# A paired SwiGLU up-projection on Trainium2: one matrix's products after the other's, and the fifth product in 512-column matmuls

## The chip, the cores and the metric

The kernel runs on one core of one Trainium2 chip. The metric is the device time of one execution in microseconds (us). The kernel before takes 1759.15 us, the median of three runs (1758.93 to 1760.65). Profiles and traces are of single executions. The engines are named as in the profile: PE (TensorE matmuls), PEld (its weight loads), DVE (VectorE), ACT (ScalarE), POOL (GpSimd) and SP (the queue that issues most DMAs).

## The reference

A decoder of two layers on 512 tokens of width 1024, all in float32. Each layer is a half-step feed-forward (FFN), a token mixer, a second half-step FFN and a norm:

```python
def swiglu(x, w1, w3, w2):
    return (jax.nn.silu(x @ w1) * (x @ w3)) @ w2
...
    for l in range(DEPTH):
        h = x + 0.5 * swiglu(rms_norm(x, ffn1_norm[l]), ffn1_w1[l], ffn1_w3[l], ffn1_w2[l])
...
        h = h + y @ w_out[l]

        h = h + 0.5 * swiglu(rms_norm(h, ffn2_norm[l]), ffn2_w1[l], ffn2_w3[l], ffn2_w2[l])

        x = rms_norm(h, final_norm[l])
```

There are four FFNs; w1 and w3 are 1024 x 2816, w2 is 2816 x 1024. The change touches the products `x @ w1` and `x @ w3` of the four FFNs only.

## The kernel before

**Precision.** Every float32 operand is cut into a high part and a low part, and a product is made of three: high x high, high x low, low x high. For a weight tile `split` (L147) does this: ACT copies the tile into the high part `whi` (L148), and DVE subtracts that from the tile and writes the low part `wlo` (L149).

**Blocks and quarters.** The 2816 hidden columns are 22 blocks of 128, f = 0 to 21. `ffn` (L475) does blocks 0 to 3 plainly. From block 4 on, two blocks are made at once by `up_pair` (L362), for w1 and w3 (i = 0 and 1) together. The blocks form quarters of 6, 6, 6 and 4; after a quarter's blocks (and one pair of the next quarter, made ahead) come its products with w2 (L546 to L564), which run from `mm` banks and add into `h`. Back to back stand therefore the pairs 4 and 6; 8, 10 and 12; 14, 16 and 18; and 20 alone. Pair 4 is called the first pair here (`f == PLAIN`).

**Seven products.** For a pair, one matrix's four quarter products (two blocks of columns, two halves of the 1024 rows, the tokens in halves of 256) are had from seven products instead of eight, over sums of weights and of operands. `Seven` (L297) holds the operand sums, once per FFN: in the traces' names `mh` and `ml` are those of products 1, 2 and 6, `xhi` those of 3 and 5, `xlo` those of 7 and 4. On the weights' side product 1 and 2 use the raw block f, 6 and 3 use sums of it, 7 and 5 use `X`, and 4 uses the raw block f + 1 (`z`).

- `X` (`wsum` in the traces) is loaded by SP (L369), and GpSimd then adds a second part into it with an accumulating DMA (L370). There are three `wsum` buffers and three `raw` buffers.
- `raw[i]` becomes the weights of 6 and 3 by two DVE additions in place (L443, L444 in the later pairs; L416, L417 in the first). The first of them reads `X[i]`.
- `unit` (L357) splits a tile that is used twice. `whi` and `wlo` have four buffers each.

**Two ways to write one product.** `product` (L377) makes 12 matmuls of 256 columns: for each of four k, the weight's high part with the operand's high part and then its low part; then four of the weight's low part. `beside` (L384) lets the operand's high and low parts, which lie side by side, pass in one matmul of 512 columns, four of these, then four of 256 columns for the weight's low part. It leaves two partial sums of 256 columns in a bank, which DVE adds (`summed`, L402). The later pairs make 2, 3, 7 and 4 with `beside`, and 1, 6 and 5 with `product`.

**Banks.** The eight PSUM banks are in named pools: `mm` 3, `cf` 1, `po` 2, `pt` 2. In the first pair products 1, 2, 6 and 5 are in two `po` banks (`xy`), and 3, 7 and 4 in two `pt` banks (`zv`). In a later pair products 1, 6 and 5 of each matrix share a `pt` bank (`x`), 2 and then 7 and 4 are in `po`, 3 in `cf` or `mm`. ACT copies products 1, 6 and 5 out of their bank into `part`.

**Order.** Each engine runs its instructions in order. A scheduler sets the order of each engine from the program and its own model; `queued` and `tc.issue_after` bind single places. In the code, a later pair makes 1 and 2 of both matrices (with each one's raw sums right behind), then 6 and 3 of both, then 7 and 5 of both, then 4 of both.

Of the kernel before, what the change touches and what calls it, by code (L numbers as in the profile page):

```python
# [13 lines left out]
AF = mybir.ActivationFunctionType  # L14
# [4 lines left out]
P = 128  # L19
D = 1024  # L20
S = 512
# [44 lines left out]
def trunk(ctx: ExitStack, tc: tile.TileContext, xT, memT, pos, w1a, w3a, w2a, w1b, w3b, w2b,  # L66
          wconv, wqk, wvm, wmem, wout, gains, small, rows, consts, out):
    nc = tc.nc
    V, G, A, T = nc.vector, nc.gpsimd, nc.scalar, nc.tensor
# [21 lines left out]
    def bank(shape, tag):  # L91

        if tag == "mm":
            return ps_mm.tile(shape, F32, tag=tag, name=tag)
        return ps_ax.tile(shape, F32, tag=tag, name=tag, bufs=1 if tag == "cf" else 2)

    def tm(name, tag="t", bufs=None):
        return tmp.tile([P, S], F32, tag=tag, name=name, **({"bufs": bufs} if bufs else {}))
# [4 lines left out]
    def raw_tile(src, cols):  # L103
        raw = wst.tile([P, UNIT], F32, tag="raw", name="raw", bufs=3)
        nc.sync.dma_start(raw[:, 0:cols], src)
        return raw
# [5 lines left out]
    first = []  # L112
# [34 lines left out]
    def split(hi, lo, x, on):  # L147
        a = A.activation(hi, x, AF.Copy)  # L148
        return a, on.tensor_tensor(out=lo, in0=x, in1=hi.bitcast(F32), op=ALU.subtract)  # L149
# [12 lines left out]
    def pair():  # L162
        return (wst.tile([P, UNIT], F32R, tag="whi", name="whi"), wst.tile([P, UNIT], F32R, tag="wlo", name="wlo"))
# [23 lines left out]
    def blk(k, n=P):  # L187
        return slice(k * n, (k + 1) * n)
# [97 lines left out]
    QW = 512  # L286
    QT = 256
# [65 lines left out]
    def gated():  # L353
        p = gated_pair()
        return [at(p, ALL, i, ALL) for i in range(2)]

    def unit(x):  # L357
        p = pair()
        split(p[0], p[1], x, V)
        return p  # L360

    def up_pair(l, w13, f, M):  # L362

        raw = [raw_tile(w13[i][l, f], D) for i in range(2)]
        X = []
        for i in range(2):

            x = wst.tile([P, UNIT], F32, tag="aux", name="wsum", bufs=3)
            nc.sync.dma_start(x.rearrange("p (f c) -> p f c", f=2), w13[i][l, f : f + 2, :, 0:QW].rearrange("f p c -> p f c"))  # L369
            G.dma_start(x, w13[i][l, f + 1], accum_op=ALU.add)  # L370
            X.append(x)
        z = wst.tile([P, UNIT], F32, tag="raw", name="raw", bufs=3)
        for i in range(2):
            nc.sync.dma_start(z[:, blk(i, QW)], w13[i][l, f + 1, :, QW:])
        x0, x1 = blk(0, QT), blk(1, QT)

        def product(ps, w, half, j, first=False):  # L377


            for n, (part, q) in enumerate([(0, q) for k in range(4) for q in ((k, 0), (k, 1))] + [(1, (k, 0)) for k in range(4)]):  # L380
                tail[0] = T.matmul(ps, w[part][:, blk(4 * half + q[0])], M.m[j][q[0]][:, q[1]], skip_group_check=True,  # L381
                                   start=first and not n, stop=n == 11)

        def beside(ps, w, half, j, first=False):  # L384


            def go(out, part, n):
                for k in range(4):
                    tail[0] = T.matmul(out, w[part][:, blk(4 * half + k)], M.m[j][k][:, 0:n], skip_group_check=True,  # L389
                                       start=first and not part and k == 0, stop=part == 1 and k == 3)  # L390

            go(ps, 0, 2)
            go(ps[:, 0], 1, 1)

        u, g = (tmp.tile([P, 2, S], F32, tag=t, name=t, bufs=n) for t, n in (("u", 1), ("g", 2)))
        part = [tm("part", "sq", 2) for _ in range(2)]
        to = (u, g)

        def add(out, a, b):
            V.tensor_tensor(out=out, in0=a, in1=b, op=ALU.add)  # L400

        def summed(out, ps, a):  # L402
            add(out, ps[:, 0], a)
            add(out, out, ps[:, 1])

        if f == PLAIN:
            xy = [bank([P, S], "po") for _ in range(2)]
            zv = [bank([P, S], "pt") for _ in range(2)]
            for i in range(2):
                w = unit(raw[i])  # L410
                product(xy[i][:, x0], w, 0, 1, first=True)
                product(xy[i][:, x1], w, 1, 2)
                A.activation(part[i], xy[i], AF.Copy)
                add(to[i][:, 0, x0], part[i][:, x0], part[i][:, x1])

                add(raw[i][:, 0:QW], raw[i][:, 0:QW], X[i][:, QW:])  # L416
                add(raw[i][:, QW:], raw[i][:, QW:], raw[i][:, 0:QW])  # L417
            for i in range(2):
                w = unit(raw[i])
                product(xy[i][:, x0], w, 0, 6)  # L420
                A.activation(part[i][:, x1], xy[i][:, x0], AF.Copy)
                product(zv[i][:, x0], w, 1, 3, first=True)
            for i in range(2):
                w = unit(X[i])
                product(xy[i][:, x0], w, 1, 5)
                A.activation(part[i][:, x0], xy[i][:, x0], AF.Copy)
                product(zv[i][:, x1], w, 0, 7)
                add(to[i][:, :, x1], zv[i].rearrange("p (n t) -> p n t", n=2), part[i][:, x0].unsqueeze(1).to_broadcast([P, 2, QT]))
            w = unit(z)
            for i in range(2):  # L430
                product(zv[i][:, x1], w, i, 4)
                add(to[i][:, 1, x0], zv[i][:, x1], part[i][:, x1])
        else:
            x = [bank([P, QT], "pt") for _ in range(2)]
            for i in range(2):
                w = unit(raw[i])
                product(x[i], w, 0, 1, first=True)
                A.activation(part[i][:, x0], x[i], AF.Copy)
                y = bank([P, 2, QT], "po")
                beside(y, w, 1, 2, first=True)  # L440
                summed(to[i][:, 0, x0], y, part[i][:, x0])

                add(raw[i][:, 0:QW], raw[i][:, 0:QW], X[i][:, QW:])  # L443
                add(raw[i][:, QW:], raw[i][:, QW:], raw[i][:, 0:QW])  # L444
            c, v = [bank([P, 2, QT], t) for t in ("cf", "mm")], []
            for i in range(2):
                w = unit(raw[i])
                product(x[i], w, 0, 6)
                A.activation(part[i][:, x1], x[i], AF.Copy)
                beside(c[i], w, 1, 3, first=True)  # L450
            for i in range(2):
                w = unit(X[i])
                v.append(bank([P, 2, QT], "po"))
                beside(v[i], w, 0, 7, first=True)
                A.activation(to[i][:, 1, x1], v[i][:, 0], AF.Copy)
                add(to[i][:, 1, x1], to[i][:, 1, x1], v[i][:, 1])
                product(x[i], w, 1, 5)
                A.activation(part[i][:, x0], x[i], AF.Copy)
                summed(to[i][:, 0, x1], c[i], part[i][:, x0])
                add(to[i][:, 1, x1], to[i][:, 1, x1], part[i][:, x0])  # L460
            w = unit(z)
            for i in range(2):
                beside(v[i], w, i, 4)
                summed(to[i][:, 1, x0], v[i], part[i][:, x1])
        out = gated()
        for n, sign in enumerate((1.0, -1.0)):
            A.activation(u[:, n], u[:, n], AF.Silu, scale=sign)
        M.gated = V.tensor_tensor(out=g, in0=g, in1=u, op=ALU.mult)
        for n, sign in enumerate((1.0, -1.0)):
            hi, lo = out[n]  # L470
            A.activation(hi, g[:, n], AF.Copy, scale=sign)
            V.scalar_tensor_tensor(out=lo, in0=g[:, n], scalar=sign, in1=hi.bitcast(F32), op0=ALU.mult, op1=ALU.subtract)  # L472
        return out

    def ffn(l, w13, w2, x, sums, factors, last, at_product, aside=None, closing=None):  # L475
# [60 lines left out]
        for q, (f0, nf) in enumerate(QUARTERS):  # L536
            ahead = 2 if q + 1 < len(QUARTERS) else 0
            for f in range(f0, f0 + nf + ahead, 2):
                if f not in g:
                    g[f], g[f + 1] = up_pair(l, w13, f, M)  # L540
                    if f == PLAIN:
                        with tc.issue_after(M.gated.ins):
                            rescale = after()
# [614 lines left out]
    for l in range(L):  # L1158
        x, new = nxt.x, Stat("st")
# [163 lines left out]
```

## Time and profile before

| | before |
|---|---|
| median of three runs | 1759.15 us |
| the profiled execution's own time | 1760.35 us |
| its span | 1758.5 us |
| mean granted clock of PE | 0.998 |
| POOL busy, share of the span | 196.0 us (11%) |
| mean rate of DMA | 144 GB/s |
| hardware DMA queue (SP): packets, MB, share | 77200, 190.45, 34.8% |
| software DMA queue (GpSimd): packets, MB, share | 19008, 61.35, 19.5% |

A row of a timeline has the start and the duration in us, the engine, the line, the operation, the tiles written and read, the count of instructions that it groups, and in brackets the idle time just ahead with what released it. `L400` is the line of the helper `add`, so additions are told apart by tiles: `raw<-raw,wsum` is the raw sum that reads X, `g<-g,po` the second addition of a `summed`. `u` belongs to the first matrix, `g` to the second. All matmuls here have weights of 128 x 128.

### The profile page before, as it was taken

To read this page: it belongs to the slowest core of one execution; us is meant where nothing else is said; L and a number is where in the kernel's file an instruction comes from. 1 tells how busy PE (TensorE), PEld (TensorE's weight loads), DVE (VectorE), ACT (ScalarE), POOL (GpSimd) and SP (SyncE) were. 2 spreads that over 40 slices of the span, in tenths; PEclk is the share of its full clock that TensorE was granted. 3 is DMA by queue.
4 is the path that set the end of the run, shared out by engine and by line. 5 is a ranking of instruction groups with operands and counts; after the bars stand their busy time and mean duration, and the time that the engine had idled before them with its cause. 6 is when DMAs were issued, how large, how long until landed. Compare 5 with 4: busy or idle time off the path is not lost.

```text
span 1758.5 us, 26405 instructions
## 1 busy us (share of the span) xinstructions
PE 1742.3 (99%) x10004; PEld 1524.0 (87%) x10004; DVE 1370.0 (78%) x2218; ACT 907.7 (52%) x1437; POOL 196.0 (11%) x220
## 2 busy tenths in 40 slices
PE   9999999999999999999999999999999999999997
PEld 7889889888888989898889898988888889898986
DVE  7969878689877868686778787776898768686866
ACT  6546445356765535353656354544567655453533
POOL 1001000006121000000010010000251210000000
PEclk9999999999999999999999999999999999999999
DMA  9456646257247546565566465542671666464632
GB/s 286 112 167 169 179 121 161 73 159 164 86 93 183 142 134 163 143 161 146 150 149 162 150 168 156 158 142 71 162 165 54 136 152 181 131 168 133 153 99 84
DMA packets 96335, 253.49 MB, mean 144 GB/s; under 512 B 9808, under 2 KB 16208, under 8 KB 96208
## 3 DMA queue, kind: packets, MB, share of 16 engines
q1 hardware_dynamic: 77200, 190.45, 34.8%
q0 software_dynamic: 19008, 61.35, 19.5%
q8 instruction: 79, 1.29, 0.3%
q14 instruction: 48, 0.39, 0.1%
HBM read 249.67 MB, written 2.10 MB: 143 GB/s over the span
## 4 chain that ended last, share of the span: by engine, by line
PE 92%; DVE 4%; DMA 2%; issue 1%; ACT 0%; SPq 0%; DVEq 0%; POOLq 0%; ACTq 0%
PE pt L381 16%; PE mm L180 14%; PE mm L182 14%; PE mm L181 14%; PE po L389 13%; PE po L381 2%; PE mm L389 2%; PE cf L389 2%; PE po L180 2%; PE po L182 2%; PE po L181 2%; PE po L928 2%; DMA wsum<-in_w3a 1%; PE mm L876 1%; PE cf L182 1%
## 5 line engine op out<-in xcount | busy, mean ns | idle before, releaser
L148 ACT ACTIVATE whi<-raw 128x1024 fp32r<-128x1024 f32 (+3 forms) x346 | 326.3, 947 | 429.1 <-PE mm L181 202.7
L149 DVE TENSOR_TENSOR wlo<-raw,whi 128x1024 fp32r<-128x1024 f32 (+3 forms) x346 | 374.7, 1088 | 99.4 <-ACT whi L148 98.2
L181 PE MATMUL mm<-glo,whi 128*128 128x512 f32 (+1 forms) x752 | 292.2, 389 | 0.0
L180 PE MATMUL mm<-ghi,whi 128*128 128x512 f32 (+1 forms) x752 | 292.0, 390 | 0.0
L182 PE MATMUL mm<-ghi,wlo 128*128 128x512 f32 (+1 forms) x734 | 285.3, 389 | 0.0
L564 DVE SCALAR_TENSOR_TENSOR h<-mm,h 128x512 f32<-128x512 f32 x126 | 86.3, 688 | 112.2 <-PE mm L182 111.8
L180 PEld LDWEIGHTS mm<-ghi,whi 128*128 128x128 f32 x752 | 141.2, 188 | 29.2 <-DVE h L564 1.2
L181 PEld LDWEIGHTS mm<-glo,whi 128*128 128x128 f32 x752 | 141.3, 188 | 28.4 <-DVE glo L472 0.2
L182 PEld LDWEIGHTS mm<-ghi,wlo 128*128 128x128 f32 x734 | 137.9, 188 | 27.7
L389 PE MATMUL po<-xlo,whi 128*128 128x512 f32 x512 | 139.5, 394 | 0.9 <-DVE g L400 0.9
L1058 DVE SCALAR_TENSOR_TENSOR there<-ypad,par,there 128x512 f32<-128x512 f32 x180 | 136.0, 779 | 1.3
L389 PEld LDWEIGHTS po<-xlo,whi 128*128 128x128 f32 x512 | 89.6, 189 | 15.2 <-DVE g L400 1.8
L180 PE MATMUL mm<-xhi,whi 128*128 128x512 f32 x256 | 101.6, 398 | 0.0
L182 PE MATMUL mm<-xhi,wlo 128*128 128x512 f32 x256 | 99.9, 390 | 0.0
L181 PE MATMUL mm<-xlo,whi 128*128 128x512 f32 x256 | 99.6, 389 | 0.0
L149 DVE TENSOR_TENSOR wlo<-wsum,whi 128x1024 fp32r<-128x1024 f32 x72 | 87.5, 1215 | 0.3 <-ACT whi L148 0.3
L389 PEld LDWEIGHTS po<-xlo,wlo 128*128 128x128 f32 x512 | 78.3, 188 | 10.6
L148 ACT ACTIVATE whi<-wsum 128x1024 fp32r<-128x1024 f32 x72 | 76.2, 1058 | 19.2 <-PE po L389 15.9
L381 PE MATMUL pt<-xhi,whi 128*128 128x256 f32 x576 | 81.9, 283 | 0.0
L389 PE MATMUL po<-xlo,wlo 128*128 128x256 f32 x512 | 81.2, 280 | 0.0
L381 PEld LDWEIGHTS pt<-xhi,whi 128*128 128x128 f32 x576 | 74.8, 190 | 0.5
L381 PE MATMUL pt<-ml,whi 128*128 128x256 f32 x512 | 72.9, 282 | 0.0
(397 smaller groups left out, 3605.7 us busy)
## 6 DMA issues: line engine op xcount, KB each, us to landing
raw<-in_w2a SPq DMA_DIRECT2D x48, 384.0 KB, 3.8
raw<-in_w2b SPq DMA_DIRECT2D x48, 384.0 KB, 3.7
raw<-in_w1a SPq DMA_DIRECT2D x26, 512.0 KB, 3.5
raw<-in_w3a SPq DMA_DIRECT2D x26, 512.0 KB, 3.7
raw<-in_w1b SPq DMA_DIRECT2D x26, 512.0 KB, 3.5
raw<-in_w3b SPq DMA_DIRECT2D x26, 512.0 KB, 3.6
wsum<-in_w1a SPq DMA_DIRECT2D x18, 512.0 KB, 4.5
wsum<-in_w3a SPq DMA_DIRECT2D x18, 512.0 KB, 3.6
```

The source lines that it names most:

```text
L148: a = A.activation(hi, x, AF.Copy)
L149: return a, on.tensor_tensor(out=lo, in0=x, in1=hi.bitcast(F32), op=ALU.subtract)
L180: T.matmul(ps, a[0], b[0], start=first, stop=False, **more)
L181: T.matmul(ps, a[0], b[1], start=False, stop=False, **more)
L182: tail[0] = T.matmul(ps, a[1], b[0], start=False, stop=last, **more)
L381: tail[0] = T.matmul(ps, w[part][:, blk(4 * half + q[0])], M.m[j][q[0]][:, q[1]], skip_group_check=True, start=first and not n, stop=n == 11)
L389: tail[0] = T.matmul(out, w[part][:, blk(4 * half + k)], M.m[j][k][:, 0:n], skip_group_check=True, start=first and not part and k == 0, st ...
L564: added = V.scalar_tensor_tensor(out=h[:, d, :], in0=ps, scalar=0.5, in1=h[:, d, :], op0=ALU.mult, op1=ALU.add)
L876: tail[0] = T.matmul(pp[i][:, z, :], q, k, start=not masked, stop=True, skip_group_check=True)
L928: tail[0] = T.matmul(po[:, 2 * c + i, :], ptb[:, i, j, :], v, start=(j == 0), stop=(j == nk - 1))
L1058: V.scalar_tensor_tensor(out=cv[:, c, :], in0=ypad[:, c, j : j + S], scalar=conv_w[:, c, j : j + 1], in1=cv[:, c, :], op0=ALU.mult, op1=AL ...
```

## The change

Four edits. First, in the later pairs the loop over the products 6 and 3 and the loop over 7 and 5 are one: for each matrix the raw sums, 6 and 3, the split of X, 7 and 5 follow on each other. Second, a matrix's raw sums move from behind products 1 and 2 into that loop, and the one that reads X is issued after the DVE operation of the last split that was written ahead of it (`unit.at`). Third, the fifth product is written with `beside`, into a `pt` bank that is now full (two partial sums of 256 columns); ACT copies the one out, and a new DVE addition adds the other. Fourth, in the first pair the two pools of banks are exchanged.

```diff
     def unit(x):
         p = pair()
-        split(p[0], p[1], x, V)
+        unit.at = split(p[0], p[1], x, V)[1]
         return p
...
         if f == PLAIN:
-            xy = [bank([P, S], "po") for _ in range(2)]
-            zv = [bank([P, S], "pt") for _ in range(2)]
+            xy = [bank([P, S], "pt") for _ in range(2)]
+            zv = [bank([P, S], "po") for _ in range(2)]
...
         else:
-            x = [bank([P, QT], "pt") for _ in range(2)]
+            x = [bank([P, 2, QT], "pt") for _ in range(2)]
             for i in range(2):
                 w = unit(raw[i])
-                product(x[i], w, 0, 1, first=True)
-                A.activation(part[i][:, x0], x[i], AF.Copy)
+                product(x[i][:, 0], w, 0, 1, first=True)
+                A.activation(part[i][:, x0], x[i][:, 0], AF.Copy)
                 y = bank([P, 2, QT], "po")
                 beside(y, w, 1, 2, first=True)
                 summed(to[i][:, 0, x0], y, part[i][:, x0])
-
-                add(raw[i][:, 0:QW], raw[i][:, 0:QW], X[i][:, QW:])
-                add(raw[i][:, QW:], raw[i][:, QW:], raw[i][:, 0:QW])
             c, v = [bank([P, 2, QT], t) for t in ("cf", "mm")], []
             for i in range(2):
+                with tc.issue_after(unit.at.ins):
+                    add(raw[i][:, 0:QW], raw[i][:, 0:QW], X[i][:, QW:])
+                add(raw[i][:, QW:], raw[i][:, QW:], raw[i][:, 0:QW])
                 w = unit(raw[i])
-                product(x[i], w, 0, 6)
-                A.activation(part[i][:, x1], x[i], AF.Copy)
+                product(x[i][:, 0], w, 0, 6)
+                A.activation(part[i][:, x1], x[i][:, 0], AF.Copy)
                 beside(c[i], w, 1, 3, first=True)
-            for i in range(2):
                 w = unit(X[i])
                 v.append(bank([P, 2, QT], "po"))
                 beside(v[i], w, 0, 7, first=True)
                 A.activation(to[i][:, 1, x1], v[i][:, 0], AF.Copy)
                 add(to[i][:, 1, x1], to[i][:, 1, x1], v[i][:, 1])
-                product(x[i], w, 1, 5)
-                A.activation(part[i][:, x0], x[i], AF.Copy)
+                beside(x[i], w, 1, 5)
+                A.activation(part[i][:, x0], x[i][:, 0], AF.Copy)
+                add(part[i][:, x0], part[i][:, x0], x[i][:, 1])
                 summed(to[i][:, 0, x1], c[i], part[i][:, x0])
                 add(to[i][:, 1, x1], to[i][:, 1, x1], part[i][:, x0])
```

How the order of the engines changes is shown at three places. The first is PE in the last pair (blocks 20 and 21) of the last FFN, where no products with w2 come between: `mm<-xhi` is the third product of the second matrix, `pt<-ml` the sixth product, `po<-xlo` a seventh or fourth, `pt<-xhi` a fifth. Before:

```order
L389 MATMUL cf<-xhi,wlo 128x256 x4
L381 MATMUL pt<-ml,whi 128x256 x8
L381 MATMUL pt<-ml,wlo 128x256 x4
L389 MATMUL mm<-xhi,whi 128x512 x4
L389 MATMUL mm<-xhi,wlo 128x256 x4
L389 MATMUL po<-xlo,whi 128x512 x4
L389 MATMUL po<-xlo,wlo 128x256 x4
L381 MATMUL pt<-xhi,whi 128x256 x8
L381 MATMUL pt<-xhi,wlo 128x256 x4
```

And after:

```order
L389 MATMUL cf<-xhi,wlo 128x256 x4
L389 MATMUL po<-xlo,whi 128x512 x4
L389 MATMUL po<-xlo,wlo 128x256 x4
L381 MATMUL pt<-ml,whi 128x256 x5
L389 MATMUL pt<-xhi,whi 128x512 x4
L389 MATMUL pt<-xhi,wlo 128x256 x4
L381 MATMUL pt<-ml,whi 128x256 x3
L381 MATMUL pt<-ml,wlo 128x256 x4
L389 MATMUL mm<-xhi,whi 128x512 x4
L389 MATMUL mm<-xhi,wlo 128x256 x4
```

The first matrix's seventh and fifth products now stand ahead of the second matrix's sixth and third, and the fifth is eight matmuls in the place of twelve.

The second place is DVE between the second and the third of three pairs in the second layer's first FFN, with buffer numbers: `raw` with `wsum` is the raw sum that reads X, `wlo<-wsum` X's split. Before:

```order
L149 TENSOR_TENSOR wlo_10074<-raw_10054,whi_10073 128x1024
L400 TENSOR_TENSOR g_9842<-g_9842,po_9894 128x256
L400 TENSOR_TENSOR u_9841<-cf_9907,part_9843 128x256
L400 TENSOR_TENSOR raw_10054<-raw_10054,wsum_10058 128x512
L149 TENSOR_TENSOR wlo_10104<-raw_10056,whi_10103 128x1024
L400 TENSOR_TENSOR u_9841<-u_9841,po_9963 128x256
L400 TENSOR_TENSOR u_9841<-u_9841,cf_9907 128x256
L400 TENSOR_TENSOR raw_10054<-raw_10054 128x512
L400 TENSOR_TENSOR g_9842<-mm_9908,part_9844 128x256
L400 TENSOR_TENSOR raw_10056<-raw_10056,wsum_10061 128x512
```

After, from the raw sum of the third pair's first matrix on (`wsum_9944` is that matrix's X, `wsum_9947` the other's):

```order
L400 TENSOR_TENSOR u_9733<-u_9733,po_9828 128x256
L149 TENSOR_TENSOR wlo_10020<-raw_9940,whi_10019 128x1024
L400 TENSOR_TENSOR g_9734<-g_9734,po_9883 128x256
L149 TENSOR_TENSOR wlo_10045<-wsum_9944,whi_10044 128x1024
L400 TENSOR_TENSOR raw_9942<-raw_9942,wsum_9947 128x512
L468 TENSOR_TENSOR g_9734<-g_9734,u_9733 128x1024
L400 TENSOR_TENSOR raw_9942<-raw_9942 128x512
```

Before, both raw sums stood ahead of either X's split; now the first matrix's X is split ahead of the second's raw sum, which comes behind the previous pair's last small additions.

The third place is PE where the first pair runs into the next, in the second layer's first FFN: `pt<-xlo` is a seventh or fourth product of the first pair, and `po<-mh`, `po<-ml` are the next pair's second. Before:

```order
L381 MATMUL pt<-xlo,whi 128x256 x7
L381 MATMUL pt<-xlo,wlo 128x256 x4
L389 MATMUL po<-mh,wlo 128x256 x2
L389 MATMUL po<-ml,wlo 128x256 x2
L389 MATMUL po<-mh,whi 128x512 x2
L389 MATMUL po<-ml,whi 128x512 x2
L381 MATMUL pt<-xlo,whi 128x256
L389 MATMUL po<-mh,wlo 128x256 x2
```

After, with the first pair's products 3, 7 and 4 in `po` banks:

```order
L381 MATMUL po<-xlo,whi 128x256 x7
L381 MATMUL po<-xlo,wlo 128x256 x4
L381 MATMUL pt<-mh,whi 128x256 x8
L381 MATMUL pt<-mh,wlo 128x256 x4
L381 MATMUL pt<-mh,whi 128x256 x8
L381 MATMUL po<-xlo,whi 128x256
L381 MATMUL pt<-mh,wlo 128x256 x4
L381 MATMUL po<-xlo,whi 128x256 x8
```

Between the first pair's last products now stand the next pair's first products (`pt<-mh`), where its second products stood before.

## The prediction

> **What bounds the kernel now.** I read the engine table first, then the chain that ended last, then the busy times of the stretches in which pairs run.
>
> ```profile
> span 1758.5 us, 26405 instructions
> PE 1742.3 (99%) x10004; PEld 1524.0 (87%) x10004; DVE 1370.0 (78%) x2218; ACT 907.7 (52%) x1437; POOL 196.0 (11%) x220
> PE 92%; DVE 4%; DMA 2%; issue 1%; ACT 0%; SPq 0%; DVEq 0%; POOLq 0%; ACTq 0%
> ```
>
> PE is busy for 99% of the span and is 92% of the chain. So a microsecond of matmuls saved is a microsecond saved, as long as the other engines keep up; and all other work counts only where PE stops for it. Two questions remain: how much PE work goes, and where PE stops before and after. The second is asked of the stretches, in which the columns are time, then busy time and instruction count of PE, PEld, DVE, ACT and POOL, clock, DMA share and GB/s. The sum is over 16 windows, which hold all 36 pairs; five of them hold all the idle time of PE.
>
> ```profile
> 53.90:103.80 49.90, 48.69 (x338) 44.92 (x337) 42.26 (x62) 28.20 (x43) 3.45 (x4) 1.00 0.66 171
> 138.20:212.20 74.00, 73.32 (x467) 66.15 (x466) 65.57 (x141) 41.21 (x70) 8.90 (x8) 1.00 0.67 171
> 234.90:299.10 64.20, 64.20 (x430) 59.19 (x429) 52.00 (x84) 35.55 (x57) 4.31 (x5) 1.00 0.62 167
> 742.80:807.80 65.00, 64.44 (x430) 59.05 (x429) 50.69 (x83) 34.39 (x55) 5.20 (x6) 1.00 0.69 178
> 924.20:969.60 45.40, 44.85 (x328) 42.30 (x327) 38.54 (x56) 26.45 (x41) 3.45 (x4) 1.00 0.66 172
> 1009.80:1075.80 66.00, 65.10 (x433) 59.35 (x432) 55.77 (x95) 38.38 (x65) 7.67 (x8) 1.00 0.65 174
> sum 789.40, PE 785.50 PEld 725.72 DVE 637.37 ACT 438.99 POOL 60.85; mean PE 49.09 PEld 45.36 DVE 39.84 ACT 27.44 POOL 3.80
> ```
>
> The clock is 1.00 throughout, so no term here is a matter of the throttle. PE stands idle for 789.40 - 785.50 = 3.9 us in all pairs together. DVE is second: in a typical three-pair stretch (234.90) it has 52.00 us of work in 64.20. So waits before can give little, and spare DVE time is about 12 us in each such stretch.
>
> **The change, part by part.**
>
> *The fifth product.* Both shapes stand in the trace side by side, since products 3, 4, 7 and the second one already go the new way. PE's timeline in the first FFN:
>
> ```profile
> 87.90 1.12 PE L381 MATMUL pt<-xhi,whi 128*128 128x256 f32 x8
> 88.86 0.64 PE L381 MATMUL pt<-xhi,wlo 128*128 128x256 f32 x4
> 89.34 0.40 PE L180 MATMUL mm<-ghi,whi 128*128 128x512 f32 x1
> 89.58 0.40 PE L181 MATMUL mm<-glo,whi 128*128 128x512 f32 x1
> 89.81 1.08 PE L389 MATMUL po<-xlo,whi 128*128 128x512 f32 x4
> 90.73 0.64 PE L389 MATMUL po<-xlo,wlo 128*128 128x256 f32 x4
> 91.20 1.12 PE L381 MATMUL pt<-xhi,whi 128*128 128x256 f32 x8
> ```
>
> The first two rows are a fifth product of today: from 87.90 to the next start at 89.34 is 1.44 us for 12 matmuls, 0.12 each. The fifth and sixth rows are the new form, four matmuls of 512 columns and four of 256: 89.81 to 91.20 is 1.39 us. Starts are used, not durations, because neighbouring records overlap. The saving is 0.05 at this place; over other places the first form takes 1.42 to 1.44 and the second 1.38 to 1.40, so 0.03 to 0.06, and I take 0.045. How often: the sum of a raw tile with an X tile stands twice in every pair.
>
> ```profile
> L400 DVE TENSOR_TENSOR raw<-raw,wsum 128x512 f32<-128x512 f32 x72 | 49.4, 686 | 21.3 <-DMA wsum<-in_w3b 11.6 <-DMA wsum<-in_w3a 5.2 <-issue 3.1
> L400 DVE TENSOR_TENSOR u<-u,po 128x256 f32<-128x256 f32 x96 | 39.8, 414 | 5.0 <-ACT u L455 3.9
> L149 DVE TENSOR_TENSOR wlo<-raw,whi 128x1024 fp32r<-128x1024 f32 x206 | 250.9, 1219 | 48.6 <-ACT whi L148 48.0
> ```
>
> 72 / 2 = 36 pairs, less the 4 first pairs (one per FFN), which keep the old form: 32 pairs x 2 matrices = 64 fifth products. 64 x 0.045 = **2.9 us** less PE work (1.9 to 3.8).
>
> A sentence apart: the Trainium skill, "TensorE: Matmul & The Clock Gate", section "Back-to-back issue gap", gives the gap between warm isolated matmuls as N/2.4 + 2.5 ns, so an estimate from it is 109 ns at 256 columns and 216 at 512, 0.01 us saved per product and 0.64 us in all; the sum would be 1757.1 by it, and 1754.8 by the rows. The trace's gaps at 256 columns, 120 ns, speak against it here.
>
> *The extra addition.* The new form leaves two partial sums, so DVE gets one more 128x256 addition with an operand in PSUM each time. The second row above has that operation at 414 ns: 64 x 0.414 = 26.5 us of DVE work. It lies beside matmuls. Per three-pair stretch it is 6 x 0.414 = 2.5 us, and 52.00 becomes 54.5 of about 64: covered on average, and I cost it at nothing there. If the cover went, all of it would come out: that is the slower rival below.
>
> *The waits.* The record understates them, since consecutive matmul records overlap: where the trace shows 0.37 or 0.56 us of idle time below, starts slip by about 0.65 and 0.83. With stops too short to show I count each window's idle time about twice: 2.4, 1.4, 0.8 (its one stop, measured), 1.1 and 1.8, together **7.5 us** before.
>
> The largest single stop is in the second layer's first FFN:
>
> ```profile
> 1037.07 1.22 DVE L149 TENSOR_TENSOR wlo<-wsum,whi 128x1024 fp32r<-128x1024 f32 x1
> 1038.32 0.38 SPq L369 DMA_DIRECT2D wsum<-in_w3a  x1
> 1042.82 0.86 POOL L370 DMA_DIRECT2D wsum<-in_w3a  x1 [16.37 <-DVE wlo L149]
> wsum<-in_w3a POOLq DMA_DIRECT2D x18, 512.0 KB, 7.4
> 1051.00 0.69 DVE L400 TENSOR_TENSOR raw<-raw,wsum 128x512 f32<-128x512 f32 x1 [3.12 <-issue]
> 1051.29 1.09 PE L389 MATMUL cf<-xhi,whi 128*128 128x512 f32 x4
> 1052.75 1.21 PE L389 MATMUL po<-xlo,whi 128*128 128x512 f32 x4 [0.37 <-DVE g L400]
> 1055.70 0.70 PE L389 MATMUL po<-mh,whi 128*128 128x512 f32 x2 [0.48 <-DVE u L400]
> ```
>
> The split of X (ends 1038.29) frees a wsum buffer; SP loads into it at 1038.32, GpSimd adds the second half at 1042.82, and by the median 7.4 us that lands near 1050.2. The addition behind it keeps DVE standing for 3.12 us, and the additions queued behind that one free PSUM banks which PE wants at 1052.75 and 1055.70. (Counted at starts: about 0.65 and 1.0.) The change moves two things here. Matrix 1's X is split right after its raw sum, ahead of matrix 2's raw sum, so SP's load and GpSimd's accumulation on their queues go out some 1 to 2 us sooner. And the addition that waits now stands behind that split, so less is queued behind it. I expect the stop to go, 1.8 to 0.2. Late next would be the second matrix's split.
>
> At the end of the second three-pair stretch of layer 0's second FFN DVE holds a small addition behind a weight split that waits for ACT:
>
> ```profile
> 804.83 0.96 DVE L149 TENSOR_TENSOR wlo<-raw,whi 128x768 fp32r<-128x768 f32 x1 [4.33 <-ACT whi L148]
> 805.23 0.39 PE L181 MATMUL mm<-glo,whi 128*128 128x512 f32 x1
> 805.71 0.41 DVE L400 TENSOR_TENSOR g<-g,po 128x256 f32<-128x256 f32 x1
> 806.17 1.19 PE L389 MATMUL po<-xlo,whi 128*128 128x512 f32 x4 [0.56 <-DVE g L400]
> ```
>
> In the new order the addition stands ahead of that split, so this goes: 0.8 to 0. In the two windows where the first pair meets the next I expect little: 2.4 to 2.6 in the first FFN, and half of 1.1 left in the second layer. The rows on the second FFN say why it may grow:
>
> ```profile
> 592.67 1.00 PE L381 MATMUL pt<-xlo,whi 128*128 128x256 f32 x7
> 597.60 1.21 DVE L149 TENSOR_TENSOR xlo<-msum,xlo 128x1024 fp32r<-128x1024 f32 x1
> 599.16 1.11 PE L381 MATMUL pt<-xlo,whi 128*128 128x256 f32 x8
> ```
>
> The operand of product 4 is ready at 598.81 and used at 599.16, a margin of 0.35 us; with the banks swapped product 4 comes sooner on PE than the next pair's fillers, so some 0.3 us may show in each of two places, 0.6. The second first-layer window (138.20) is full of other DVE work:
>
> ```profile
> 173.00:197.00 24.00, 23.32 (x154) 20.92 (x153) 24.00 (x47) 13.33 (x23) 2.59 (x3) 1.00 0.69 170
> ```
>
> DVE has no free time there at all, so four or so extra additions can cost up to 1.7 us, and the shorter order may give as much back; I take 1.4 to 1.3.
>
> One wait is new: a fifth product's bank (pt) now comes free with a DVE addition, not with ACT's copy alone, and the next pair's first product waits for it in PE's order, with every matmul behind it. No row shows this wait; its lower bound is a gain of zero, its upper one 0.414 us in each of the 20 places where pair follows pair, 8.3 us; the DVE slack of 52.00 in 64.20 is nearest to nothing, and I take **0.8**. Waits after: 0.2 + 0 + 2.6 + 0.6 + 0.6 + 1.3 + 0.8 = 6.1, that is **1.4 us** less.
>
> *Sum.* 1758.5 - 2.9 - 1.4 = 1754.2 of span. The profiled run took 1760.35, 1.85 more than its span, so 1756.05; the median 1759.15 lies 1.2 under that run, so **1754.8 us**.
>
> **The rivals.**
>
> *Stops only change places.* The DVE extra and the release of banks give back what the two stops yield. For it: DVE is full in 173 to 197, and the margin of 0.35. Against: both stops have a named cause that goes. It gives 1759.15 - 2.9 + 0 to 1.5 = 1756.2 to 1757.7, no change that can be told: a measurement here tells 0.2%, 3.5 us.
>
> *PE counts columns alone.* Then 12 x 256 = 4 x 512 + 4 x 256 = 3072 columns and the first term is nothing. Against it stands 1.44 beside 1.39 in one timeline. 1759.15 - 1.4 = 1757.7. The estimate from the page of the Trainium skill named above is nearly this rival, at 1757.1.
>
> *All stops go.* With X split early, every place shown keeps its lead: work of 2.9 to 3.8 and about 4.5 to 5 of the 7.5 us gone, 1751.
>
> *Slower: DVE becomes the bound where pair follows pair.* The third pair of a stretch lives off a lead that the earlier ones build:
>
> ```profile
> 1653.13 0.69 DVE L400 TENSOR_TENSOR raw<-raw,wsum 128x512 f32<-128x512 f32 x1 [3.18 <-DMA wsum<-in_w3b]
> 1654.73 1.22 DVE L149 TENSOR_TENSOR wlo<-raw,whi 128x1024 fp32r<-128x1024 f32 x1
> 1656.37 0.64 PE L381 MATMUL pt<-ml,wlo 128*128 128x256 f32 x4
> ```
>
> The low part is ready at 1655.95 and used at 1656.37, a margin of 0.42, and the group row of that split has it 206 times. One pair has two more additions, 0.83 us, on DVE. From the point at which the margin is under 0.83 and the wait for the accumulating DMA (3.18 here) does not shrink, each of the 8 three-pair stretches stops PE by about 0.83: 6.6 - 2.9 = 3.7 slower, 1763. Against: that wait is itself spare DVE time, and in the new order it stands behind work that needs no DMA.
>
> **How the numbers follow.** Forecast 0.49, its own range 1753.3 to 1756.3; changed places 0.27; columns alone 0.05; all stops 0.09; slower 0.10. The range reaches to 1751.0, the work's larger bound with the stops gone, and to 1760.0, half of the slower mechanism; beyond lie about 0.15. Faster by over 0.2% means under 1755.6: 0.09 and most of the forecast's 0.49, 0.53. Slower: 0.10. Within: the rest, 0.37.
>
> **What would show it.** The fifth product at 1.39 us from start to start, PE's busy total 2 to 4 us lower, DVE's 26 higher. At the third pair of the second layer's first FFN no wait of over 0.3 us on PE, and no 4 us wait of a weight split ahead of `g<-g,po`. Wrong would be: PE idle in the 16 windows above 3.9 us, with releasers `part` or `wlo` on DVE in third pairs; or products that take 1.44 in either form.

## The result, and the profile after

| | before | after |
|---|---|---|
| median | 1759.04 us (4 runs) | 1777.88 us (4 runs, 1776.48 to 1779.5) |
| ratio to before, 95% interval | 1 | 1.0106 [1.0088, 1.0123] |
| span of the profiled execution | 1758.5 us | 1774.7 us |
| mean granted clock of PE | 0.998 | 0.997 |

The kernel became 18.8 us slower where 4.3 us faster was forecast. The page of the profile after, with its counts, busy times and chain:

```profile
span 1774.7 us, 25901 instructions
PE 1745.1 (98%) x9748; PEld 1511.2 (85%) x9748; DVE 1386.3 (78%) x2282; ACT 907.2 (51%) x1437; POOL 199.4 (11%) x220
PE 86%; DVE 7%; DMA 3%; ACT 1%; issue 1%; POOL 0%; SPq 0%; DVEq 0%; ACTq 0%; POOLq 0%
```

256 matmuls and as many weight loads are gone (64 x 4), DVE has 64 instructions more. But PE's share of the chain fell from 92% to 86%, and DVE's and DMA's rose: PE now waits. Its waits, summed by waiting line and releaser (us in total, times, the longest):

```profile
PE mm L180 <- ACT whi L148: 9.7, 6, 2.3
...
PE po L381 <- DVE xlo L149: 1.2, 2, 0.7
PE mm L180 <- ACT ghi L471: 1.1, 4, 0.3
PE po L389 <- DVE g L400: 1.1, 1, 1.1
...
PE po L389 <- DVE ypad L616: 1.1, 1, 1.1
```

The first row did not exist before: at the start of a stage of products with w2, PE's matmul on the second w2 tile waits for its split on ACT. The six places are at 94.2, 204.5, 623.6, 972.5, 1078.9 and 1499.6 us: behind pair 6 in all four FFNs, and behind pair 12 in the first FFN of both layers, where DVE also has mixer work.

How the loss divides can be counted from start to start, as an estimate. If a 512-column matmul gets 0.227 us, one of 384 columns 0.174 and one of 256 columns 0.118, then what passes beyond that up to the next start, over all matmuls of these widths in the program, adds up to 31.7 us before and 50.1 us after. So stops cost 18.4 us more. The spans of the two profiled executions differ by 1774.7 - 1758.5 = 16.2 us, so the work itself became 16.2 - 18.4 = -2.2 us, that is 2.2 us shorter. Of the 50.1 us, the six stops are 10.7 and slow matmuls behind one of them 1.7 (see the last section); seven stops of 0.4 to 1.2 us in the first layer's first FFN, from 85 to 196 us, are 5.2, where before three in that part were 1.2.

Where no stop falls the change does what it should. Windows of two three-pair stretches after, with the columns of the windows above:

```profile
241.00:304.10 63.10, 63.10 (x402) 57.12 (x401) 53.31 (x90) 34.77 (x56) 4.33 (x5) 1.00 0.63 169
...
752.40:815.40 63.00, 63.00 (x402) 57.04 (x400) 53.29 (x90) 34.70 (x56) 5.22 (x6) 1.00 0.68 182
```

And of the first two pairs of the first layer's second FFN, with the stop at 623.6, and of the three pairs of the second layer's first FFN that end with the stop at 1078.9:

```profile
584.60:630.90 46.30, 44.02 (x313) 41.04 (x313) 38.90 (x57) 26.26 (x41) 3.46 (x4) 1.00 0.63 160
1019.90:1088.40 68.50, 66.08 (x408) 59.14 (x407) 57.90 (x101) 37.77 (x66) 8.23 (x8) 0.98 0.66 174
```

In the first two PE has no idle time; in the second two it has 2.3 and 2.4 us, and in the last one the mean clock is 0.98. One stop, followed back: the timeline after of DVE, then of SP, ACT and PE, in the first layer's second FFN behind pair 6.

```profile
609.83 1.22 DVE L149 TENSOR_TENSOR wlo<-wsum,whi 128x1024 fp32r<-128x1024 f32 x1
610.97 0.69 DVE L400 TENSOR_TENSOR raw<-raw,wsum 128x512 f32<-128x512 f32 x1
...
614.92 1.23 DVE L149 TENSOR_TENSOR wlo<-raw,whi 128x1024 fp32r<-128x1024 f32 x1
616.18 0.33 SPq L105 DMA_DIRECT2D raw<-in_w2b  x1
617.31 0.38 SPq L369 DMA_DIRECT2D wsum<-in_w1b  x1
618.44 6.48 SPq L105 DMA_DIRECT2D raw<-in_w2b  x3
622.73 0.84 ACT L148 ACTIVATE whi<-raw 128x768 fp32r<-128x768 f32 x1 [4.68 <-DMA raw<-in_w2b]
623.63 0.50 PE L180 MATMUL mm<-ghi,whi 128*128 128x512 f32 x1 [2.29 <-ACT whi L148]
```

DVE first splits the first matrix's X (609.83); only behind it stands the second matrix's raw sum (610.97), since the change binds it there. The split of that summed tile ends at 616.15 and frees one of the three `raw` buffers; SP's load of the second w2 tile, which waits for that buffer, goes out at 616.18. Two more splits follow at once, so an X load and the next w2 load go out at 617.31 and 618.44, beside this one. The chain of waits has the transfer from 616.18 to 622.63, 6.45 us; ACT splits the tile, and PE has stood since 621.3. Before, the sum and the split of the second raw tile stood ahead of X's split, and the same load had more lead (DVE, then SP):

```profile
598.74 0.68 DVE L400 TENSOR_TENSOR raw<-raw,wsum 128x512 f32<-128x512 f32 x1
...
602.77 1.23 DVE L149 TENSOR_TENSOR wlo<-raw,whi 128x1024 fp32r<-128x1024 f32 x1 [0.24 <-ACT whi L148]
...
605.05 1.22 DVE L149 TENSOR_TENSOR wlo<-wsum,whi 128x1024 fp32r<-128x1024 f32 x1
600.58 3.77 SPq L105 DMA_DIRECT2D raw<-in_w2b  x2
```

SP's row groups two loads, the second of which goes out at 604.02, as the second raw tile's split ends, 8.4 us ahead of PE's first w2 product at 612.38. After, PE's first w2 product is at 620.71, 4.5 us behind the second load. The lead is not all of it: run 13 has the same 4.5 us and no stop, and is compared with this place below.

### The profile page after: what moved, and what is told of

Read it like the earlier page. It is cut to its first block, busy times and chain, and to the rows that moved or that the text cites. A ratio compares the mean times of both kernels' runs of the same rounds, so it can differ in the third digit from the quotient of the medians.

```text
span 1774.7 us, 25901 instructions
## 1 busy us (share of the span) xinstructions
PE 1745.1 (98%) x9748; PEld 1511.2 (85%) x9748; DVE 1386.3 (78%) x2282; ACT 907.2 (51%) x1437; POOL 199.4 (11%) x220
## 4 chain that ended last, share of the span: by engine, by line
PE 86%; DVE 7%; DMA 3%; ACT 1%; issue 1%; POOL 0%; SPq 0%; DVEq 0%; ACTq 0%; POOLq 0%
PE mm L180 14%; PE mm L182 13%; PE mm L181 13%; PE po L389 12%; PE pt L381 10%; PE pt L389 4%; PE mm L389 2%; PE cf L389 2%; DVE wlo L149 2%; PE po L180 2%; PE po L182 2%; PE po L181 2%; PE po L928 2%; PE po L381 1%; DMA raw<-in_w2a 1%
## 5 line engine op out<-in xcount | busy, mean ns | idle before, releaser
L381 PE MATMUL pt<-ml,whi 128*128 128x256 f32 x608 | 87.7, 283 | 0.3 <-ACT whi L148 0.3
L381 PE MATMUL pt<-mh,whi 128*128 128x256 f32 x608 | 85.8, 283 | 0.0
L381 PEld LDWEIGHTS pt<-ml,whi 128*128 128x128 f32 x608 | 79.7, 191 | 1.2 <-ACT whi L148 0.5
```

## The experiments

Each is compared with the kernel before on the same chip. The ratio is the one on record, with its 95% interval; it is not the quotient of the two medians, which for run 9 is 1.0050. Theory A at the outset: the fused order frees the `raw` buffer late. Rival B: the 64 additions put DVE behind. Rival C: the exchanged banks.

**1. The fifth product undone in the changed kernel.**

```diff
-                beside(x[i], w, 1, 5)
+                product(x[i][:, 0], w, 1, 5)
                 A.activation(part[i][:, x0], x[i][:, 0], AF.Copy)
-                add(part[i][:, x0], part[i][:, x0], x[i][:, 1])
```

> The changed kernel with the fifth product written with 12 matmuls of 256 columns again and without its extra addition; fused loops, moved raw sums and exchanged banks stay. Theory A (release order: the second matrix's raw tile is summed and split behind the first matrix's X split, so its buffer and with it the second w2 load at the start of a w2 stage come late): still slow, 1772 to 1780 us, and PE waits of over 1 us for ACT's whi on the first w2 products stay in at least four of six places. Rival B (the 64 extra DVE additions put DVE behind): back to 1758 to 1762 us with those waits gone.

1777.02 us, 1.0104 [1.0086, 1.0123]. The waits for w2's whi stay: 9.4 us in 5. Without any extra addition the kernel is as slow, so B is not what slows this kernel.

**2. The fifth product alone on the kernel before.**

```diff
-                product(x[i], w, 1, 5)
-                A.activation(part[i][:, x0], x[i], AF.Copy)
+                beside(x[i], w, 1, 5)
+                A.activation(part[i][:, x0], x[i][:, 0], AF.Copy)
+                add(part[i][:, x0], part[i][:, x0], x[i][:, 1])
```

> The kernel before with the fifth product alone changed (eight matmuls, a full pt bank, one more addition each). Theory A: 1756 to 1759 us, since release order is that of before and the matmuls save 2 to 3 us. Rival B: 1766 to 1775 us. No wait of PE on a w2 product's whi of over 0.5 us under A, several under B.

1777.82 us, 1.0113 [1.0096, 1.013]: against A's number, and as slow as the whole change, but by another stop. PE's and DVE's largest new waits, and the place in the first FFN (DVE's timeline, then PE's):

```profile
PE po L389 <- DVE g L400: 10.0, 7, 2.5
DVE raw L400 <- issue: 26.1, 9, 4.8
276.85 0.69 DVE L400 TENSOR_TENSOR raw<-raw,wsum 128x512 f32<-128x512 f32 x1 [3.11 <-issue]
277.46 0.41 DVE L400 TENSOR_TENSOR g<-g,po 128x256 f32<-128x256 f32 x1
277.93 1.19 PE L389 MATMUL po<-xlo,whi 128*128 128x512 f32 x4 [0.89 <-DVE g L400]
```

In third pairs DVE stands for the accumulating load of X, as before: the profile calls the wait "issue", but the accumulation into this X landed at 276.77 by the trace, and such a landing stands within 0.1 us ahead of each of the nine sums. The addition that frees PE's next `po` bank now stands behind the waiting raw sum; before, it stood ahead (it ran at 272.46, the sum at 275.48). This is the place of the prediction's slower rival, which had the split of the next weights late there and not this addition, and it has another price.

**3. The changed kernel with the loops apart again.** The sums stay moved and bound, the fifth product and the banks stay changed.

```diff
                 beside(c[i], w, 1, 3, first=True)
+            for i in range(2):
                 w = unit(X[i])
```

> The changed kernel with the fused loop cut in two again (6 and 3 of both matrices, then 7 and 5 of both); the raw sums stay moved and bound to the last split, the fifth product and the banks stay changed. Theory A: 1756 to 1764 us, the waits for w2's whi gone, since the second matrix's raw tile is split ahead of both X splits. Rival B: 1770 us or more. Rival C (the exchanged banks of the first pair delay the join and everything behind it): 1768 us or more, with the waits in the first quarters alone.

1755.28 us, 0.9975 [0.9966, 0.9985], the fastest version of all. The waits for w2's whi are gone, and so are DVE's for the X load. One line turns 1.0106 into 0.9975; rivals B and C fall as causes of this loss.

**4. The changed kernel with the first pair's banks as before** (`xy` in `po`, `zv` in `pt`).

> The changed kernel with the first pair's banks as before. Theory A: 1773 to 1778 us, the join's waits for xlo (1.0 and 0.65 us) go and the others stay. Rival C: 1765 us or less, the waits in the first quarter of each FFN gone (6 to 8 us of loss lie there).

1774.28 us, 1.0092 [1.0075, 1.0109]. The waits on w2's whi stay, 7.5 us in 6. C is not the cause. The waits for xlo at the joins (where the first pair meets the next) were expected to go; they did not, and are 1.5 us in 2 where the changed kernel has 1.2 in 2.

**5. The moved and bound sums alone on the kernel before** (loops apart, fifth product and banks as before).

```diff
-                add(raw[i][:, 0:QW], raw[i][:, 0:QW], X[i][:, QW:])
-                add(raw[i][:, QW:], raw[i][:, QW:], raw[i][:, 0:QW])
             c, v = [bank([P, 2, QT], t) for t in ("cf", "mm")], []
             for i in range(2):
+                with tc.issue_after(unit.at.ins):
+                    add(raw[i][:, 0:QW], raw[i][:, 0:QW], X[i][:, QW:])
+                add(raw[i][:, QW:], raw[i][:, QW:], raw[i][:, 0:QW])
                 w = unit(raw[i])
```

> The kernel before with one edit: the raw sums stand behind products 1 and 2 of both matrices, the one that reads X bound to the last split. If the move takes away DVE's waits for the accumulating X load in third pairs, and these were worth little before: 1757 to 1760 us, and the fifth product is what makes the version with loops apart faster by another 2 to 3 us. Rival (the fifth product yields nothing, the moved sums everything): 1754.5 to 1756 us.

1759.94 us, 1.0003 [0.9993, 1.0013]: nothing by itself, though DVE's waits of raw sums for the X load, 16.8 us before in two rows, fell to 2.3. They had cost PE little.

**6. Loops apart (as in 3), and the banks as before.**

> The version with loops apart, with the first pair's banks as before. If the exchange of banks costs what the last comparison of the changed kernel suggests (3.6 us): 1751.5 to 1753 us. Rival (that 3.6 us was one of the order that the scheduler happened to choose): 1755 to 1757 us.

1757.48 us, 0.9992 [0.9983, 1.0], a little above the higher of the two ranges expected, and by the medians 2.2 us slower than 3. In the changed kernel the same edit came out 3.6 us faster. The banks' share has no sign of its own here; it was not followed further. Against 5, which differs by the fifth product alone, it is 2.5 us faster.

**7. The changed kernel, but the second w2 tile of each stage isn't loaded.** Its split reads a constant, so this tile's part of the result is left out; the order of DVE around these places is that of the changed kernel.

```diff
+                if d == 1:
+                    w, still = pair(), onesq.unsqueeze(1).to_broadcast([P, nf, P])
+                    hi, lo = (x[:, 0 : nf * P].rearrange("p (j c) -> p j c", j=nf) for x in w)
+                    split(hi, lo, still, V)
+                else:
+                    w = weights(w2[l, d, :, f0 * P : (f0 + nf) * P], nf * P, V)
```

> The changed kernel; the second w2 tile of each stage isn't loaded (its split, on ACT and DVE as before, reads a constant), so the second block's part of each stage is left out of the result. Theory A (the raw buffer that the second matrix's split frees, and the w2 load that waits for it): the waits on w2's whi fall from 9.7 us to under 3, the time to 1762 to 1768 us. Rival (ACT and DVE are simply behind at those places): the waits stay above 6 us, the time at 1773 us or more.

1763.04 us, 1.0029 [1.0019, 1.0039]. No wait for w2's whi is left in PE's list. Taking one transfer away gives back 1777.88 - 1763.04 = 14.8 of the 18.8 us: the wait for this load, with what follows from it, is the larger part of the loss. What stays is stops of about 1 us in the first FFN (at 76, 183 and 187 us) and 0.44 four times at the end of an FFN.

**8. The fifth product alone, without its extra addition** (the last `+` line of 2 is dropped, so the high weight part times the operand's low part is missing).

> The kernel before with the fifth product alone in 512-column matmuls and its extra addition left out, so that the product of the high weight part with the operand's low part is missing in it. If the 64 additions put DVE behind (by their time, or by what they displace): 1755 to 1760 us. Rival (the full bank or the shorter matmuls alone bring the bad order): 1768 us or more, with PE waiting for g or u additions in third pairs as in the run with the additions.

1757.61 us, 0.9984 [0.9974, 0.9994]. The additions make the 20 us of 2, not the matmuls or the full bank. PE's wait for g additions is down to 1.6 us.

**9. The changed kernel with the loops cut in the pairs 6 and 12 alone.**

> The changed kernel, with the loops cut in two in the pairs 6 and 12 alone (ahead of the first two w2 stages of each FFN, where the stops were seen) and fused in all others. If the fused order is harmful only where a w2 stage follows while DVE is behind: 1754 to 1758 us. Rival (the fused order costs everywhere, unseen in the stops): 1762 us or more.

1767.81 us (five runs, 1762.68 to 1769.17), 1.0038 [1.0024, 1.0051]: a miss. The six stops are gone, but the same chain struck a pair's weights. ACT's and PE's timeline in the second layer's first FFN:

```profile
1032.78 1.06 ACT L148 ACTIVATE whi<-raw 128x1024 fp32r<-128x1024 f32 x1 [6.77 <-DMA raw<-in_w3a]
1034.16 2.08 PE L389 MATMUL pt<-xhi,whi 128*128 128x512 f32 x4 [4.45 <-ACT part L449]
```

A load of w3 went out at 1023.91, when a split of a raw tile ended, and took 8.76 us beside four others; ACT's copy of a `pt` bank stood behind its split. So the order can do harm at a raw load elsewhere too, not only ahead of w2.

**10. Loops apart (as in 3), fused in pair 6 alone.**

> The version with loops apart, with the loop fused in pair 6 alone. Theory A: the four stops for w2's whi at the start of the first w2 stage of each FFN come back (7 us, with what follows them 7 to 10), 1762 to 1766 us. Rival: 1755 to 1757 us, the order of the other pairs is needed for the stop.

1763.39 us, 1.0022 [1.0013, 1.0031], 8.1 us above 3. The stops at the four first w2 stages come back, 5.9 us in 4 (6.6 from start to start).

**11. Loops apart (as in 3) without the binding.**

```diff
-                with tc.issue_after(unit.at.ins):
-                    add(raw[i][:, 0:QW], raw[i][:, 0:QW], X[i][:, QW:])
+                add(raw[i][:, 0:QW], raw[i][:, 0:QW], X[i][:, QW:])
```

> The version with loops apart, without the binding of the sum that reads X to the last split. If the binding is what keeps that sum from standing ahead of additions which PE waits for: 1765 us or more, DVE waits for the X load of 10 us or more in all and PE waits for g additions in third pairs, as with the fifth product alone. If the place in the code is enough: 1754 to 1757 us.

1773.24 us, 1.0078 [1.0064, 1.0092]. DVE's raw sums wait 21.0 us in 6 ("issue" again, each with the landing of an X load just ahead), PE for g additions for 9.6 us in 8, the stop of run 2. With the loops apart and the additions in, the binding is what avoids it.

**12. Fused loops, the raw sums where they were before, unbound.**

```diff
                 summed(to[i][:, 0, x0], y, part[i][:, x0])
+                add(raw[i][:, 0:QW], raw[i][:, 0:QW], X[i][:, QW:])
+                add(raw[i][:, QW:], raw[i][:, QW:], raw[i][:, 0:QW])
             c, v = [bank([P, 2, QT], t) for t in ("cf", "mm")], []
             for i in range(2):
-                with tc.issue_after(unit.at.ins):
-                    add(raw[i][:, 0:QW], raw[i][:, 0:QW], X[i][:, QW:])
-                add(raw[i][:, QW:], raw[i][:, QW:], raw[i][:, 0:QW])
                 w = unit(raw[i])
```

> The changed kernel with fused loops, but the raw sums of both matrices written behind products 1 and 2 as before, unbound. Theory A (what counts is where the second matrix's raw tile is split): 1770 us or more, with the waits for w2's whi. Rival (what counts is where it is summed): 1755 to 1765 us without them.

1755.85 us, 0.998 [0.9971, 0.9989], without the waits. Theory A as it was put falls: the fused order is not harmful in itself. What counts is when the second matrix's tile is summed. The theory left: the binding holds that sum behind the first X's split. Two runs try it.

**13. The changed kernel, the second matrix's sum bound to the split of the first raw tile.**

```diff
-                with tc.issue_after(unit.at.ins):
+                with tc.issue_after((mine if i else unit.at).ins):
                     add(raw[i][:, 0:QW], raw[i][:, 0:QW], X[i][:, QW:])
                 add(raw[i][:, QW:], raw[i][:, QW:], raw[i][:, 0:QW])
                 w = unit(raw[i])
+                mine = unit.at
```

> The changed kernel with one edit: the second matrix's raw sum is bound to the split of the first matrix's raw tile, no longer to the split of its X. If that binding is the whole loss: 1754 to 1757 us, no waits on w2's whi over 0.5 us. Rival (the fused order itself, whatever the sum is bound to, costs where DVE is behind): 1765 us or more, with those waits.

1758.74 us, 1.0003 [0.9994, 1.0012]. DVE's and SP's timeline at the place shown above for the changed kernel:

```profile
602.78 0.69 DVE L400 TENSOR_TENSOR raw<-raw,wsum 128x512 f32<-128x512 f32 x1
...
604.31 1.22 DVE L149 TENSOR_TENSOR wlo<-wsum,whi 128x1024 fp32r<-128x1024 f32 x1
...
606.58 1.22 DVE L149 TENSOR_TENSOR wlo<-raw,whi 128x1024 fp32r<-128x1024 f32 x1
607.83 0.33 SPq L105 DMA_DIRECT2D raw<-in_w2b  x1
```

The sum stands ahead of X's split again, and the waits for w2's whi are gone. The load goes out at 607.83, but 616.18 is not the time to set beside it, since everything comes earlier here: PE's first w2 product is at 612.28, so the lead is 4.5 us in both kernels. Counted from the stage's first w2 load (608.28 in the changed kernel, 602.89 here), three things differ. The second load goes out 7.9 us behind it in the changed kernel and 4.9 here, 3.0 us later. It takes 6.45 us there and 4.4 here, 2.0 longer. And PE would take up the second tile at 621.2 there, right behind its first two w2 matmuls, and does so at 616.95 here, behind other products: 12.9 and 14.1 us behind the first load, 1.2 sooner. Together 6.2 us: PE's matmul on the second tile, which starts 2.5 us late there, has by this count some 3.7 us to spare here. All three come with this one edit; what each is worth alone no run shows. The time is 1.7 us above the top of the range expected: two stops of 1.2 us are left in the first FFN's second stretch, at 149.9 (DVE ypad) and 185.7 (a u addition).

**14. The changed kernel without any binding.**

> The changed kernel without the binding, the sums staying where the change writes them. If the binding is the loss and the fused order by itself keeps the X load from holding up DVE: 1754 to 1757 us. Rival (without it DVE waits for the X load in third pairs, as with the fifth product alone): 1768 us or more, with PE waits for g additions.

1756.04 us, 0.9986 [0.9977, 0.9995]. Neither stop appears; a raw sum of DVE waits 1.0 us once. So the binding, in the fused order, is the whole loss: without it the changed kernel is 2.2 us faster than the kernel before in these runs.

## Why the prediction was wrong

**The step that failed** is in the part on the waits: "Matrix 1's X is split right after its raw sum, ahead of matrix 2's raw sum, so SP's load and GpSimd's accumulation on their queues go out some 1 to 2 us sooner." The step moves matrix 2's raw sum back to bring X's split forward. The prediction followed the buffer that comes free sooner (`wsum`) and not the one that comes free later: `raw`, which the next weights, those of w2, wait for. It even named "the second matrix's split" as late next, and put that at nothing in the sum. The runs put the wait for w2's second load, with what follows from it, at 14.8 of the 18.8 us (run 7). At the place shown, that load goes out 3.0 us later than in run 13, takes 2.0 longer beside the loads that go out with it, and is wanted 1.2 sooner. The order that the binding makes was taken for a cure, as it is with the loops apart (11 against 3); in the fused order it is the fault, and 13 and 14 show the loss gone with it. The prediction's sign of being wrong, more than 3.9 us of idle time of PE in the stretches of pairs, came true, but with ACT's whi as the releaser and not `part` or `wlo` on DVE.

**The fifth product** was right in kind and a little large: 2.9 us were forecast. By the medians from start to start it takes 1.433 us before (26 places where its 12 matmuls stand together) and 1.401 after (64), which is 64 x 0.032 = 2.0 us; between runs 5 and 6 it is 2.5. (The 2.2 us of the count above follows from the widths' times that it takes for granted.) One of the new form in the changed kernel's own PE timeline takes 625.58 - 624.20 = 1.38 us:

```profile
624.20 1.07 PE L389 MATMUL pt<-xhi,whi 128*128 128x512 f32 x4
625.11 0.64 PE L389 MATMUL pt<-xhi,wlo 128*128 128x256 f32 x4
625.58 0.40 PE L182 MATMUL mm<-ghi,wlo 128*128 128x512 f32 x1
```

So PE does not count columns alone, and that rival falls. The estimate of 0.64 us from the Trainium skill's page "TensorE: Matmul & The Clock Gate", section "Back-to-back issue gap", falls too: the runs show three to four times that.

**The extra addition** was costed at nothing because DVE had 54.5 us of work in about 64. By busy share it is free: in the two quiet windows above DVE has 53.3 of 63.1 and PE never stops. In the old order it is not: 20 us between runs 2 and 8. A share says how much time is free, not where; the additions moved the one that frees a bank behind a wait of DVE. The slower rival had the place of run 2 (third pairs, the X load) and undersized it: 0.83 us for each stretch, where single stops reached 2.5 us. In the changed kernel itself it did not come.

**The X load.** The stop of the third pair was forecast to go from 1.8 to 0.2, and it went: no wait of a raw sum for a transfer is left after. The stop at 806 went too. The run with the moved sums alone shows how little this was worth: 1.0003. The waits before were sized too large, too: at 1052.75 and 806.17 the starts are 0.53 and 0.72 us late by the count above, not 0.65 and 0.83, and the stops of over 0.15 us in the five windows add up to some 6 us, not 7.5.

**The joins.** Forecast 2.6 us in the first FFN, and new stops of 0.3 in two others. After, 74.95 and 76.08 have 0.31 and 0.74 us of idle time there, and the second layer's first FFN 0.49; none is seen in the second FFNs. Near enough.

**The sum and the range.** Without the harmful combination the time comes near the 1754.8 us forecast (runs 3, 12 and 14: 1755.28, 1755.85, 1756.04). That is in part luck: against the kernel before beside them these runs are 4.3, 3.2 and 2.2 us faster, and the fifth product gives 2.0 to 2.5 of it where 2.9 was forecast. The range failed because the one mechanism that it held on the slow side was another one, with a price of 0.83 us a place.

## What to carry to other kernels

When a change brings one buffer's last reader forward, list what goes back in the same queue, and which load waits for that one's buffer: a tile whose last read comes 3 us later delays the transfer that refills it by as much, buffers that come free together send their loads out side by side, and the stop may come in a later stage. When two kernels are compared at one place, count from an event that both have there, not from the start of the program: of the 8.4 us between 607.83 and 616.18, 5.4 were there already at the stage's first load. An ordering edge that cures a stop in one order (run 3 against 11) can be the cause of one in another (the changed kernel against 14), so test each edge with each order. And a busy share of 85% is no cover for an instruction that is put into an in-order queue ahead of something urgent.

## What the runs showed of the hardware

A stop can cost more than its length. Windows of the changed kernel around two stops, each with the stretch behind it:

```profile
620.90:623.60 2.70, 0.44 (x2) 0.01 (x1) 0.00 (x0) 0.87 (x2) 0.00 (x0) 1.00 1.02 383
623.70:627.10 3.40, 3.40 (x17) 2.90 (x18) 2.25 (x5) 1.69 (x5) 0.86 (x1) 1.00 0.67 208
1075.50:1078.80 3.30, 1.07 (x8) 0.78 (x6) 1.19 (x3) 0.82 (x2) 0.00 (x0) 1.00 1.02 378
1078.90:1082.70 3.80, 3.80 (x12) 3.17 (x13) 2.15 (x5) 1.61 (x5) 0.86 (x1) 0.55 0.76 218
```

Both stops are 2.3 us of idle time. Behind the first the granted clock stays at 1.00; behind the second it is 0.55 over the 3.8 us, in which four 512-column matmuls take 1.71 us from start to start (1079.61 to 1081.32) in place of 0.91, so that this stop costs some 1.7 us more (the sum of what the starts from 1079.2 to 1082.6 are late). Run 9 had the same behind its stop of 4.45 us, and in its 3.4 us window from 1034.20 the clock was 0.50. Why one stop of 2.3 us lowers the clock and another does not, the runs don't show. The Trainium skill's page "TensorE: Matmul & The Clock Gate", section "What's actually happening", has a free-running window of about 3.4 us that decides between half and full clock. The slow stretch here, from 1079.2 to 1082.6, is as long. The section lets the half clock come after a whole idle window; here 2.3 us of idle time were enough, and the measurement decides. Whether the place of the window in time tells the two stops apart, no run here tests.

The same load takes longer beside others. The second w2 load of a stage (384 KB; the last stage of each FFN, with 256 KB, is left out) took 3.0 to 3.4 us from issue to landing in the kernel before, beside one or two other loads of weights, and 4.5 to 6.5 us in the changed kernel, beside three or four. In run 10 it took 5.5 to 5.8 us behind the four fused pairs, beside four others, and 3.0 to 3.2 us in the other stages, beside one or two. The count alone does not set it: in run 14 it took 3.0 to 4.1 us beside one to three.
